# FFN-entry tensor sums moved from GpSimd to VectorE, output-projection operands split in two tiles, and mixer C's head norm moved into its attention pipeline

## The chip, the cores and the metric

The kernel runs on one core of one Trainium2 chip. A core has five engines, each with its own in-order queue of instructions: TensorE (PE in the profile; its weight loads are PEld), VectorE (DVE), ScalarE (ACT), GpSimd (POOL) and SyncE (SP), which here issues the DMAs. Engines wait for each other by semaphores. The metric is the device time of one execution in microseconds; lower is better.

## The reference

A trunk of two post-norm layers on 1024 tokens of width 1024, in float32. Layer 0 mixes with mixer AB (dilated-window attention beside latent attention), layer 1 with mixer C (differential attention, 8 heads of width 128, each normed on its own). What matters here:

```python
o = diff_attention(q, k, v, lam)                       # mixer C
o = rms_norm(o, subln, LN_EPS) * (1.0 - lambda_init)   # per head, over its 128 values
y = o.reshape(B, S, C_MIX) @ w_out
x = layer_norm(ALPHA * x + y, ln_mix_g[i], ln_mix_b[i])
a = x @ w_gate; u = x @ w_up                           # then conv over tokens, gelu, product, w_down
```

The output is the residual stream after both layers.

## The kernel before

Every float32 product is made of three matmuls in a faster float32 format: each operand is split into a high part (a cast, on ACT or POOL) and a low part (value minus high part, on DVE), and `mm3` (L157 to L160) adds high x high, high x low and low x high in PSUM. Tokens stand in 8 tiles of 128. The stages follow one another: projections and heads of mixer AB, `out_proj(0)`, `ffn(0)`, an embedding gate, then the same for layer 1 with mixer C. The code gives an order, and a scheduler reorders instructions within it before they are put in the engines' queues; from then on each engine is in order.

*Mixer C.* `pipeline` runs 8 heads of 8 items (128 queries each). In one slot it starts an item's scores and softmax (`a`: scores s on PE, maximum on DVE, exponential on ACT at L439, combination on POOL and DVE), transposes a finished one (`b`: tiles xt, copied as pth by ACT and ptl by DVE), and after every second item multiplies a pair with the values (`c`: PSUM tile av, copied by ACT into oT, the head's transposed output of 1024 columns). Beside that, projections of the next head run (pp, then nat, ks, kt and v). PE's PSUM tiles of one bank (`bank`, tag b) rotate over four banks; scores and the pair tiles of the FFN use two tiles of two banks (`banks2`). Seven heads' oT go to DRAM (mix), the last stays in SBUF.

*Output projection.* `out_proj` goes over the token tiles. For a tile it loads seven heads (`MixTiles.seven`, tile mr), copies the last head in (`last`), and splits into mh and ml. For layer 1 it first norms: `norm` squares on ACT (sq, L893), sums over the head's 128 partitions with a matmul by ones (ss, L895), takes Ln and Exp on ACT (L896, L897) and scales on DVE (L898), in pieces of 512, 384 and 128 columns. `linear` runs 2 halves n of 8 k, 48 matmuls into two one-bank tiles po, and adds each half to the residual xn on DVE (L1069). `ln` is the layer norm (statistics and two passes on DVE, L870 to L881; two tiny steps rs and mostly the last pass, L882, on POOL). `xt.put` of the tile before transposes its normed rows on PE (xt). In the last tile `linear` calls put of tile 6 and the first weight splits amid its second half; put of tile 7 follows in `ffn`.

*FFN entry.* The two FFN products are block products of 2 x 2 blocks with seven multiplications in place of eight. They need sums of the weight blocks (s1 to s4, tile ws) and of the token blocks (t1 to t4): `Weights.sums` makes s1 and s3 on POOL always, and s2 and s4 on POOL too for the first two weights; `XSeven.put` makes t1 and the raw t2 tile by tile, and `finish` makes t3 and t4 after the last tile, with the first of two sums each on DVE and the second on POOL (128x1024). All are split again. `ffn` runs the products of the first two weights interleaved (`order`), reads the results with sums on DVE (L1158: u, c), and starts the third weight when PSUM frees. Weights come by two DMAs of 512 KB each (`load`, tiles wf).

```python
order = [(0, "a00"), (0, "a01"), (1, "a00"), (1, "a01")]
order += [(m, name) for name in ("s1", "s4", "s2", "s3", "a11") for m in range(2)]
```

Of the kernel before, what the change touches and what calls it, by code (L numbers as in the profile page):

```python
# [15 lines left out]
P = 128  # L16
NT = 8
# [14 lines left out]
def tile_hybrid_encoder(  # L32
# [294 lines left out]
    class XSeven:  # L327
# [10 lines left out]
        def put(self, t, xn):  # L338
# [3 lines left out]
            if t == 4:  # L342
                self.make("t1")
                self.make("b11")
                self.t2 = [unit("t2", [P, 2, 512]) for _ in range(2)]
            if t >= 4:
                t1 = mid2("t1", [P, 4, P])

            def put(b, pt):
                for j in range(2):  # L350
# [11 lines left out]
                    if t >= 4 and b == 1:  # L362
                        add(self.t2[j][at], src, v, ALU.subtract)
            transposed(xn, put)

        def finish(self, j, temps):

            for n in ("t2", "t3", "t4"):
                self.make(n, 1)
            h, l = ({n: x[j] for n, x in d.items() if len(x) > j} for d in (self.h, self.l))  # L370
            t2, (t3, t4) = self.t2[j], temps
# [5 lines left out]
            self.t2[j] = None  # L377

            def step():
                split_value(t3, h["t3"], l["t3"])  # L380
                split_value(t4, h["t4"], l["t4"])
            return step
# [87 lines left out]
    def pipeline(items, plan):  # L470
# [9 lines left out]
        pending = None  # L480
        for i in range(n):
# [5 lines left out]
            plan.run(i, "mid")  # L487
            if pending is not None:
                pending.c()
                pending = None  # L490
# [4 lines left out]
        pending.c()  # L495

# [90 lines left out]
    class ItemA:  # L587
# [37 lines left out]

        def c(self):
# [81 lines left out]
    class ItemB:  # L708
# [30 lines left out]
        c = ItemA.c  # L739

# [75 lines left out]
    class ItemC:  # L816
# [26 lines left out]
        def c(self):  # L843
# [6 lines left out]
            nc.scalar.copy(oT[:, q4 * 256:q4 * 256 + 256], po)  # L850
# [34 lines left out]
    class MixTiles:  # L885
# [4 lines left out]
        def norm(self, x, n):  # L890

            sq = mid2("sq", [P, n, P])
            nc.scalar.activation(sq, x, AF.Square)  # L893
            pss = blocks(bank("ss"))[:, 0:n, :]
            nc.tensor.matmul(pss, lhsT=ones, rhs=sq, start=True, stop=True)  # L895
            nc.scalar.activation(sq, pss, AF.Ln, bias=eps_ln, scale=1.0 / 128)  # L896
            nc.scalar.activation(sq, sq, AF.Exp, scale=-0.5)  # L897
            nc.vector.scalar_tensor_tensor(x, x, sub, sq, op0=ALU.mult, op1=ALU.mult)  # L898
# [12 lines left out]
        def last(self, t, oT):  # L911
            mr, mh, ml = self.m[t]
            nc.scalar.copy(mr[:, 7, :], oT[:, t * P:(t + 1) * P])
            if self.i == 1:
                self.norm(mr[:, 7:8], 1)
            split(mr[:, 7:8], mh[:, 7:8], ml[:, 7:8])
            self.m[t] = mh, ml
# [126 lines left out]
    def out_proj(i, w, mt, oT, xsrc, xt, early):  # L1044
# [14 lines left out]
        def linear(t, beside):  # L1059
            mh, ml = m.pop(t)  # L1060
            xr = xns[t]
            for n in range(2):
                sl = slice(512 * n, 512 * n + 512)
                po = bank("po")
                for k in range(NK):
                    if n == 1 and k == NK // 2:
                        beside()
                    mm3(po, mh[:, k, :], ml[:, k, :], w[k][0][:, sl], w[k][1][:, sl], k == 0, k == NK - 1)
                nc.vector.scalar_tensor_tensor(xr[:, sl], xr[:, sl], ALPHA, po, op0=ALU.mult, op1=ALU.add)  # L1069

        load(0)
        for t in range(NT):
            residual(t)
            load(t + 1)
            if t == NT - 1:
                early(0)

                def beside():
                    xt.put(t - 1, xns[t - 1])
                    early(1)  # L1080
                linear(t, beside)
            else:
                linear(t, lambda: None)
                if t:
                    xt.put(t - 1, xns[t - 1])
            ln(xns[t], t >= NT - 2)
            nc.sync.dma_start(out=xmid[i][t], in_=xns[t])
# [3 lines left out]
    class Weights:  # L1091
# [13 lines left out]
        def sums(self, eng=None):  # L1105
# [7 lines left out]
            self.v.update({"a11": a11, "s1": s1, "s2": s2, "s3": s3, "s4": s4})  # L1113

# [8 lines left out]
        def steps(self):  # L1123

            return [self.sums] + [lambda n=n: self.split(n) for n in Products.ORDER]
# [435 lines left out]
```

## Time and profile before

| | |
|---|---|
| median of 3 runs | 3123.81 us (3122.83 to 3125.05) |
| profiled execution | 3123.14 us, its span 3120.8 us |
| granted TensorE clock, mean | 0.990 |
| PE, DVE, ACT, POOL busy in the span | 97%, 74%, 38%, 35% |
| mixer C, one head | 71.0 us |
| projection 1, its first matmul to its 46th of the last tile | 2209.91 to 2323.30 us |
| entry of ffn(1), up to the first output sum u | to 2381.59 us |

The profile is of one execution. A row of a group has line, engine, operation, output and inputs, shapes and count, then busy us and mean ns of one, then the idle time before it and what ended that. A timeline row has start and length in us; a bracket gives idle time just before it and what ended it. A row of the waits has who waited for whom, total us, times, and the longest.

### The profile page before, as it was taken

The numbers are of one execution on the slowest core, as the hardware profiler recorded it, in microseconds if no ns is written. First come the engines' busy times: TensorE is split into PE (matmuls) and PEld (weight loads), VectorE is DVE, ScalarE is ACT, GpSimd is POOL, SyncE is SP. The second block draws the span as 40 slices with busy tenths as digits, with TensorE's granted clock in tenths as the row PEclk, the third lists the DMA queues.
The fourth block names the chain that finished last, engine by engine and source line by source line (L and its number), as shares of the span: only waits on it lengthen the run. The fifth ranks groups of instructions, "written<-read, shape, count | busy, mean of one in ns | idle before, by whom it ended". The sixth has DMA issues, their size and how long they took to land.

```text
span 3120.8 us, 43023 instructions
## 1 busy us (share of the span) xinstructions
PE 3014.5 (97%) x15704; PEld 2589.3 (83%) x15704; DVE 2295.5 (74%) x3850; ACT 1184.5 (38%) x2506; POOL 1084.9 (35%) x1560
## 2 busy tenths in 40 slices
PE   8999999999799999999999999999898999999999
PEld 8888989888678888888889999998676888888887
DVE  6666487875898887867638777778679888877764
ACT  5555577761232222101225555555423222211111
POOL 4444544333532221101225555554344222211112
PEclk9999999999999999999999999999999999999999
DMA  3000100044122222623111010004322222243221
GB/s 120 28 28 25 31 28 8 28 132 131 69 81 81 81 81 93 217 95 108 59 63 32 28 35 28 28 18 134 105 93 75 81 81 81 81 176 135 102 78 64
DMA packets 89250, 237.50 MB, mean 76 GB/s; under 512 B 9040, under 2 KB 32720, under 8 KB 89040
## 3 DMA queue, kind: packets, MB, share of 16 engines
q1 hardware_dynamic: 89040, 234.76, 22.0%
q8 instruction: 124, 2.03, 0.3%
q14 instruction: 86, 0.70, 0.1%
HBM read 179.15 MB, written 55.57 MB: 75 GB/s over the span
## 4 chain that ended last, share of the span: by engine, by line
PE 60%; DVE 5%; DMA 2%; POOL 2%; issue 1%; ACT 1%; SPq 0%; DVEq 0%; ACTq 0%; POOLq 0%
PE pb L160 5%; PE pb L159 5%; PE pb L158 5%; PE pd L158 5%; PE pd L159 5%; PE pd L160 5%; PE s L583 4%; PE pp L159 3%; PE pp L160 3%; PE pp L158 3%; PE pa L158 2%; PE xt L163 2%; PE pa L160 2%; PE pa L159 2%; PE pg L158 2%; PE pg L160 2%
## 5 line engine op out<-in xcount | busy, mean ns | idle before, releaser
L1363 DVE TENSOR_TENSOR xn<-xn,pd 128x512 f32<-128x512 f32 x320 | 213.1, 683 | 91.9 <-PE pd L160 90.9
L141 DVE TENSOR_TENSOR ptl<-xt,pth 128x512 fp32r<-128x512 f32 (+2 forms) x384 | 239.9, 652 | 55.4 <-ACT pth L398 38.8
L158 PE MATMUL pd<-dh,dh 128*128 128x512 f32 x704 | 274.3, 390 | 2.2 <-DVE xn L1363 2.2
L158 PE MATMUL pp<-wh,xth 128*128 128x384 f32 x768 | 266.8, 348 | 8.7 <-ACT wh L145 6.8
L159 PE MATMUL pd<-dl,dh 128*128 128x512 f32 x704 | 274.0, 389 | 0.0
L160 PE MATMUL pd<-dh,dl 128*128 128x512 f32 x704 | 273.3, 389 | 0.0
L159 PE MATMUL pp<-wl,xth 128*128 128x384 f32 x768 | 260.3, 339 | 1.6 <-DVE wl L148 1.5
L160 PE MATMUL pp<-wh,xtl 128*128 128x384 f32 x768 | 259.2, 338 | 0.0
L439 ACT ACTIVATE e<-s,nmx 128x1024 f32<-128x1024 f32 x192 | 214.4, 1118 | 96.1 <-DVE nmx L829 73.1
L324 ACT CAST w<-ws 128x512 fp32r<-128x512 f32 x132 | 81.5, 621 | 355.7 <-PE pb L160 284.1
L159 PE MATMUL pb<-xt,w 128*128 128x512 f32 x528 | 207.2, 392 | 7.2 <-DVE xt L141 7.2
L158 PE MATMUL pb<-xt,w 128*128 128x512 f32 x528 | 206.8, 392 | 0.0
L160 PE MATMUL pb<-xt,w 128*128 128x512 f32 x528 | 206.4, 391 | 0.0
L163 PE MATMUL xt<-ident,e 128*128 128x128 f32 x1440 | 193.3, 273 | 5.7 <-POOL e L732 3.0
L138 POOL TENSOR_SCALAR w<-ws 128x512 fp32r<-128x512 f32 x44 | 34.9, 794 | 426.5 <-PE pa L160 403.2
L163 PEld LDWEIGHTS xt<-ident,e 128*128 128x128 f32 x1440 | 163.2, 141 | 18.7 <-POOL e L732 4.3
L324 ACT CAST dh<-dr 128x1024 fp32r<-128x1024 f32 x44 | 46.1, 1052 | 334.7 <-DMA dr<-gated 193.4
L138 POOL TENSOR_SCALAR dh<-dr 128x1024 fp32r<-128x1024 f32 x44 | 46.3, 1054 | 355.1 <-DMA dr<-in_w_down_dram 164.3
L141 DVE TENSOR_TENSOR w<-ws,w 128x512 fp32r<-128x512 f32 x176 | 160.5, 914 | 1.5 <-ACT w L324 0.5
L158 PEld LDWEIGHTS pd<-dh,dh 128*128 128x128 f32 x704 | 132.1, 188 | 30.5 <-DVE xn L1363 3.1
L158 PEld LDWEIGHTS pp<-wh,xth 128*128 128x128 f32 x768 | 145.4, 190 | 13.8 <-ACT wh L145 7.6
L160 PEld LDWEIGHTS pd<-dh,dl 128*128 128x128 f32 x704 | 132.1, 188 | 27.6
(281 smaller groups left out, 8798.7 us busy)
## 6 DMA issues: line engine op xcount, KB each, us to landing
wf<-in_w_gate_dram SPq DMA_DIRECT2D x44, 512.0 KB, 3.9
wf<-in_w_up_dram SPq DMA_DIRECT2D x44, 512.0 KB, 4.1
gated<-c SPq DMA_DIRECT2D x44, 512.0 KB, 2.9
dr<-in_w_down_dram SPq DMA_DIRECT2D x44, 512.0 KB, 3.2
dr<-gated SPq DMA_DIRECT2D x44, 512.0 KB, 3.7
wr<-in_w_c_dram SPq DMA_DIRECT2D x32, 384.0 KB, 3.2
pes<-peo SPq DMA_DIRECT2D x64, 128.0 KB, 2.1
xmid<-xn SPq DMA_DIRECT2D x16, 512.0 KB, 2.9
```

Of the source, the lines that this page charges most:

```text
L138: nc.gpsimd.tensor_scalar(o, i, 1.0, 1.0, op0=ALU.mult, op1=ALU.mult)
L141: nc.vector.tensor_tensor(lo, src, f32(hi), op=ALU.subtract)
L158: nc.tensor.matmul(o, lhsT=lh, rhs=rh, start=start, stop=False)
L159: nc.tensor.matmul(o, lhsT=lh, rhs=rl, start=False, stop=False)
L160: nc.tensor.matmul(o, lhsT=ll, rhs=rh, start=False, stop=stop)
L163: nc.tensor.transpose(o, in_=i, identity=ident)
L324: nc.scalar.copy(h, v)
L439: nc.scalar.activation(dst, s, AF.Exp, bias=negmax, scale=1.0, accum_out=l)
L583: nc.tensor.matmul(s[:, kh * 512:kh * 512 + 512], lhsT=qt[:, hl, i, :], rhs=self.ks[kh][:, j, :], start=hl == 0, stop=hl == 1)
L1363: nc.vector.tensor_tensor(xns[t][:, sl], xns[t][:, sl], po, op=ALU.add)
```

## The change

Three parts. (1) The head norm of mixer C leaves the output projection: `ItemC.c` squares the pair's result, and a new step `d`, one slot later, sums, takes Ln and Exp and scales, 256 columns at a time, 32 times. For the other mixers' items `d` does nothing. (2) In `out_proj` the split goes into two tiles of four k (high and low side by side), the last head is split straight from oT, k is the outer loop with both halves n in one two-bank tile, one DVE addition of 1024 columns takes the place of two, and every put follows the next tile's `linear`. (3) At the FFN entry all tensor sums of the first two weights and of t3 and t4 are on DVE; t3 is made tile by tile in put; the steps are spread over other places of `order`; the load of the second weight follows the split of the first. From the third weight on nothing changes.

```diff
@@ XSeven.put @@
+                self.t3 = [unit("t3", [P, 2, 512]) for _ in range(2)]
             if t >= 4:
-                t1 = mid2("t1", [P, 4, P])
+                t1, b01 = mid2("t1", [P, 4, P]), mid2("b01", [P, 4, P])
 
             def put(b, pt):
+                if t >= 4 and b == 0:
+                    nc.scalar.copy(b01, pt)
...
                     if t >= 4 and b == 1:
                         add(self.t2[j][at], src, v, ALU.subtract)
+                        add(self.t3[j][at], src, b01[:, 2 * j:2 * j + 2, :], ALU.subtract)
...
-        def finish(self, j, temps):
-
-            for n in ("t2", "t3", "t4"):
-                self.make(n, 1)
...
-            add(t3, t2, h["b00"], ALU.subtract)
-            add(t3, t3, l["b00"], ALU.subtract, nc.gpsimd)
-            add(t4, h["b10"], t2, ALU.subtract)
-            add(t4, t4, l["b10"], ALU.add, nc.gpsimd)
-            split_value(t2, h["t2"], l["t2"])
...
+        def finish(self, name, j, temp=None):
+
+            self.make(name, 1)
+            h, l = self.h[name][j], self.l[name][j]
+            if name == "t4":
+                add(temp, self.h["b10"][j], self.t2[j], ALU.subtract)
+                add(temp, temp, self.l["b10"][j])
+                v, self.t2[j] = temp, None
+            elif name == "t3":
+                v, self.t3[j] = self.t3[j], None
+            else:
+                v = self.t2[j]
+            split_value(v, h, l)
@@ pipeline @@
             plan.run(i, "mid")
+            if ended is not None:
+                ended.d()
+                ended = None
             if pending is not None:
                 pending.c()
-                pending = None
+                pending, ended = None, pending
             items[i].b()
@@ ItemC @@
-            nc.scalar.copy(oT[:, q4 * 256:q4 * 256 + 256], po)
+            o = oT[:, q4 * 256:q4 * 256 + 256]
+            nc.scalar.copy(o, po)
+            self.sq = mid2("sq", [P, 256])
+            nc.scalar.activation(self.sq, po, AF.Square)
+
+        def d(self):
+
+            oT, sq, q4 = self.st["oT"], self.sq, self.t // 2
+            o = oT[:, q4 * 256:q4 * 256 + 256]
+            pss = bank("ss")[:, 0:256]
+            nc.tensor.matmul(pss, lhsT=ones, rhs=sq, start=True, stop=True)
+            nc.scalar.activation(sq, pss, AF.Ln, bias=eps_ln, scale=1.0 / 128)
+            nc.scalar.activation(sq, sq, AF.Exp, scale=-0.5)
+            nc.vector.scalar_tensor_tensor(o, o, sub, sq, op0=ALU.mult, op1=ALU.mult)
             if self.t == NT - 1:
                 self.st["sink"](oT)
@@ MixTiles @@
-        def norm(self, x, n):
...
-            if self.i == 1:
-                self.norm(mr[:, 0:4], 4)
-                self.norm(mr[:, 4:7], 3)
-            mh, ml = runit("mh", [P, NK, P]), runit("ml", [P, NK, P])
-            split(mr[:, 0:7], mh[:, 0:7], ml[:, 0:7])
-            self.m[t] = mr, mh, ml
+            two = [runit("mhl", [P, 2, 4, P]) for _ in range(2)]
+            for j, m in enumerate(two):
+                n = 4 - j
+                split(mr[:, 4 * j:4 * j + n], m[:, 0, 0:n], m[:, 1, 0:n])
+            self.m[t] = mr, two
 
         def last(self, t, oT):
...
+            mr, two = self.m[t]
+            x = oT[:, t * P:(t + 1) * P]
+            split(x, two[1][:, 0, 3], two[1][:, 1, 3], nc.scalar)
+            self.m[t] = [(two[k // 4][:, 0, k % 4], two[k // 4][:, 1, k % 4]) for k in range(NK)]
@@ out_proj @@
+        def linear(t, beside=None):
+
+            xr, mt_ = xns[t], m.pop(t)
+            po = banks2("po")
+            for k in range(NK):
+                if k == NK // 2 and beside:
+                    beside()
+                for n in range(2):
+                    sl = slice(512 * n, 512 * n + 512)
+                    mm3(po[:, sl], *mt_[k], w[k][0][:, sl], w[k][1][:, sl], k == 0, k == NK - 1)
+            nc.vector.scalar_tensor_tensor(xr, xr, ALPHA, po, op0=ALU.mult, op1=ALU.add)
...
+            if t < NT - 1:
+                linear(t)
+            else:
                 early(0)
...
+                linear(t, lambda: early(1))
+                ln(xns[t], True)
+                nc.sync.dma_start(out=xmid[i][t], in_=xns[t])
+            if t:
+                xt.put(t - 1, xns[t - 1])
+            if t < NT - 1:
+                ln(xns[t], t == NT - 2)
+                nc.sync.dma_start(out=xmid[i][t], in_=xns[t])
@@ Weights.sums, ffn_early @@
-            add(s1, a10, a11, ALU.add, nc.gpsimd)
-            add(s2, s1, a00, ALU.subtract, eng)
-            add(s4, a01, s2, ALU.subtract, eng)
-            add(s3, a00, a10, ALU.subtract, nc.gpsimd)
             self.v.update({"a11": a11, "s1": s1, "s2": s2, "s3": s3, "s4": s4})
+            steps = [lambda: add(s1, a10, a11, ALU.add, eng), lambda: add(s2, s1, a00, ALU.subtract),
+                     lambda: add(s4, a01, s2, ALU.subtract), lambda: add(s3, a00, a10, ALU.subtract, eng)]
+            if eng is None:
+                return steps
...
                 w[0].load()
-                w[1].load()
             else:
                 w[0].split("a00")
                 w[0].split("a01")
+                w[1].load()
@@ ffn @@
-        w[0].sums(nc.gpsimd)
...
-        w[1].sums(nc.gpsimd)
...
+                for a in range(2):
+                    sums[a] = w[a].sums()
+                    sums[a][0]()
+                    w[a].split("s1")
...
+            if n == 2:
+                for a in range(2):
+                    sums[a][1]()
+                    sums[a][2]()
+                    w[a].split("s4")
             if n == 3:
...
+                for a in range(2):
+                    xt.finish("t2", a)
+                for a in range(2):
+                    w[a].split("s2", True)
             if n == 4:
...
+                for a in range(2):
+                    xt.finish("t3", a)
+                for a in range(2):
+                    sums[a][3]()
+                    w[a].split("s3")
             if n == 5:
...
+                for a in range(2):
+                    xt.finish("t4", a, temps[a])
```

How the instructions stand: PE in mixer C, in the slot after the one that finished a pair, before (xt are transposes of attention weights, s scores, kt keys):

```order
L163 MATMUL kt_18427<-ident,nat_18314 128x128
L163 MATMUL xt_18444<-ident,e_18259 128x128 x4
L163 MATMUL xt_18451<-ident,e_18259 128x128 x4
L583 MATMUL s_18459<-ks_17358,qt_18280 128x512 x2
L583 MATMUL s_18459<-ks_17754,qt_18280 128x512 x2
L583 MATMUL s_18468<-ks_17358,qt_18280 128x512 x2
```

and now:

```order
L163 MATMUL kt_18481<-ident,nat_18367 128x128
L868 MATMUL ss_18498<-sq_18404,ones 128x256
L163 MATMUL xt_18504<-ident,e_18312 128x128 x4
L587 MATMUL s_18519<-ks_17383,qt_18333 128x512
L163 MATMUL xt_18511<-ident,e_18312 128x128 x4
L587 MATMUL s_18519<-ks_17383,qt_18333 128x512
L587 MATMUL s_18519<-ks_17788,qt_18333 128x512 x2
L587 MATMUL s_18528<-ks_17383,qt_18333 128x512 x2
```

ss, the matmul by ones, stands between kt and the transposes, and one score matmul has moved between the two transposed groups. ACT in the same slot now (nat, ks and v are copies of the projection):

```order
L546 COPY nat_18487<-pp_18456 128x256
L567 CAST ks_18265<-kt_18481 64x128
L554 CAST v_18266<-pp_18456 128x128
L869 ACTIVATE sq_18404<-ss_18498,eps_ln 128x256
L398 CAST pth_18406<-xt_18504 128x4x128
L870 ACTIVATE sq_18404<-sq_18404 128x256
L567 CAST ks_18265<-kt_18481 64x128
L398 CAST pth_18407<-xt_18511 128x4x128
```

Ln (L869) and Exp (L870) stand behind the copies of the projection and around the first copy pth. POOL at the entry of ffn(1), before (ws are weight sums, wf raw weights, w the split, rs the layer norm's two steps):

```order
L318 TENSOR_TENSOR ws_24159<-wf_24057 128x512
L874 TENSOR_SCALAR rs_24044<-mv_24043 128x1
L318 TENSOR_TENSOR ws_24160<-wf_24056,wf_24057 128x512
L875 TENSOR_TENSOR rs_24044<-rs_24044,mhalf 128x1
L318 TENSOR_TENSOR ws_24159<-ws_24159,wf_24056 128x512
L318 TENSOR_TENSOR ws_24160<-wf_24056,ws_24159 128x512
L318 TENSOR_TENSOR ws_24171<-wf_24061 128x512
L318 TENSOR_TENSOR ws_24172<-wf_24060,wf_24061 128x512
L318 TENSOR_TENSOR ws_24171<-ws_24171,wf_24060 128x512
L318 TENSOR_TENSOR ws_24172<-wf_24060,ws_24171 128x512
L138 TENSOR_SCALAR w_24168<-wf_24060 128x512
L874 TENSOR_SCALAR rs_24149<-mv_24148 128x1
```

and now, from the same place:

```order
L138 TENSOR_SCALAR w_24152<-wf_24120 128x512
L895 TENSOR_SCALAR rs_24108<-mv_24107 128x1
L896 TENSOR_TENSOR rs_24108<-rs_24108,mhalf 128x1
L138 TENSOR_SCALAR w_24228<-wf_24155 128x512
L895 TENSOR_SCALAR rs_24186<-mv_24185 128x1
L896 TENSOR_TENSOR rs_24186<-rs_24186,mhalf 128x1
L138 TENSOR_SCALAR w_24378<-ws_24246 128x512
L138 TENSOR_SCALAR w_24382<-ws_24252 128x512
```

The ws rows are gone from POOL; the norm's steps follow each other. DVE shortly ahead of the first u, now (c holds t4 for a while, xb and t token blocks and their sums):

```order
L318 TENSOR_TENSOR ws_24246<-wf_24120,wf_24121 128x512
L318 TENSOR_TENSOR ws_24252<-wf_24155,wf_24156 128x512
L318 TENSOR_TENSOR c_24301<-xb_4987_23590,t_5039_23970 128x1024
L141 TENSOR_TENSOR w_24378<-ws_24246,w_24378 128x512
L141 TENSOR_TENSOR w_24382<-ws_24252,w_24382 128x512
L318 TENSOR_TENSOR c_24301<-c_24301,xb_4989_23592 128x1024
L318 TENSOR_TENSOR c_24301<-xb_4988_23591,t_5040_23971 128x1024
L141 TENSOR_TENSOR w_24427<-wf_24121,w_24427 128x512
L141 TENSOR_TENSOR xt_5115_24401<-c_24301,xt_5114_24400 128x1024
L318 TENSOR_TENSOR c_24301<-c_24301,xb_4990_23593 128x1024
L141 TENSOR_TENSOR w_24430<-wf_24156,w_24430 128x512
L141 TENSOR_TENSOR xt_5117_24407<-c_24301,xt_5116_24406 128x1024
```

The sums s3 (first two rows) and t4 stand on DVE among the low parts (L141) of the split.

More of the change, by code (lines that the diff above doesn't have):

```diff
@@ L479, in pipeline @@
         plan.run(-1, "last")
-        pending = None
+        pending = ended = None
         for i in range(n):
@@ L487, in pipeline @@
             plan.run(i, "mid")
+            if ended is not None:
+                ended.d()
+                ended = None
             if pending is not None:
                 pending.c()
-                pending = None
+                pending, ended = None, pending
             items[i].b()
@@ L495, in pipeline @@
         pending.c()
+        pending.d()
     class Block64:
@@ L624, in make_pt @@
             return PTA(self.t)
+        def d(self):
+            pass
         def c(self):
@@ L739, in tile_hybrid_encoder @@
         c = ItemA.c
+        d = ItemA.d
     class Latent:
@@ L888, in __init__ @@
             self.i, self.m = i, {}
-        def norm(self, x, n):
[L892 to L898, printed above, removed]
         def seven(self, t):
@@ L1057, in residual @@
             nc.sync.dma_start(out=xns[t], in_=xsrc[t])
[L1059 to L1069, printed above, removed]
+        def linear(t, beside=None):
[8 more added lines that the diff above has]
+            nc.vector.scalar_tensor_tensor(xr, xr, ALPHA, po, op0=ALU.mult, op1=ALU.add)
         load(0)
@@ L1074, in out_proj @@
             load(t + 1)
-            if t == NT - 1:
+            if t < NT - 1:
+                linear(t)
+            else:
                 early(0)
[L1078 to L1087, printed above, removed]
+                linear(t, lambda: early(1))
[6 more added lines that the diff above has]
+                nc.sync.dma_start(out=xmid[i][t], in_=xns[t])
         return lambda: xt.put(NT - 1, xns[NT - 1])
@@ L1108, in sums @@
             s1, s2, s3, s4 = s12[:, 0], s12[:, 1], s34[:, 0], s34[:, 1]
-            add(s1, a10, a11, ALU.add, nc.gpsimd)
-            add(s2, s1, a00, ALU.subtract, eng)
-            add(s4, a01, s2, ALU.subtract, eng)
-            add(s3, a00, a10, ALU.subtract, nc.gpsimd)
             self.v.update({"a11": a11, "s1": s1, "s2": s2, "s3": s3, "s4": s4})
+            steps = [lambda: add(s1, a10, a11, ALU.add, eng), lambda: add(s2, s1, a00, ALU.subtract),
+                     lambda: add(s4, a01, s2, ALU.subtract), lambda: add(s3, a00, a10, ALU.subtract, eng)]
+            if eng is None:
+                return steps
+            for step in steps:
+                step()
         HI = {"s3", "a01", "a11"}
@@ L1123, in steps @@
         def steps(self):
-            return [self.sums] + [lambda n=n: self.split(n) for n in Products.ORDER]
+            return [lambda: self.sums(nc.gpsimd)] + [lambda n=n: self.split(n) for n in Products.ORDER]
     class Products:
@@ L1294, in ffn @@
         order += [(m, name) for m in range(2, NF) for name in Products.ORDER]
-        w[0].sums(nc.gpsimd)
+        sums = [None] * 2
         w[1].split("a00", False)
         w[1].split("a01", False)
-        w[1].sums(nc.gpsimd)
-        first = [None] * 2
         todo = []
@@ L1303, in ffn @@
             pr[m].product(name)
-            if n == 1:
+            if n == 0:
                 c00 = unit("c00", [P, 2, 512])
@@ L1307, in ffn @@
                     pr[a].go_ahead(c00[:, a])
-                w[0].split("s1")
-                w[1].split("s1")
-            if n == 2:
+                for a in range(2):
+                    sums[a] = w[a].sums()
+                    sums[a][0]()
+                    w[a].split("s1")
+            if n == 1:
                 late()
                 new_c()
-                c2 = late_c[0]
-                first[0] = xt.finish(0, [c2[:, a, :].rearrange("p (k q) -> p k q", k=2) for a in range(2)])
+                temps = [late_c[0][:, a, :].rearrange("p (k q) -> p k q", k=2) for a in range(2)]
+            if n == 2:
[3 more added lines that the diff above has]
+                    w[a].split("s4")
             if n == 3:
-                w[0].split("s4")
-                w[1].split("s4")
-                w[0].split("s2", True)
-                w[1].split("s2", True)
+                for a in range(2):
+                    xt.finish("t2", a)
+                for a in range(2):
+                    w[a].split("s2", True)
             if n == 4:
-                first[1] = xt.finish(1, [unit("t", [P, 2, 512]) for _ in range(2)])
+                for a in range(2):
[3 more added lines that the diff above has]
+                    w[a].split("s3")
             if n == 5:
-                w[0].split("s3")
-                first[0]()
-                w[1].split("s3")
-                first[1]()
+                for a in range(2):
+                    xt.finish("t4", a, temps[a])
             if n == 6:
```

14 lines of the change are left out of this document (1 added, 13 removed).

## The prediction

> **What bounds the kernel now.** I read the page first (busy shares, the chain that ended last), then the busy time by stretch, then the waits of TensorE (PE) around the two places that the change touches, and then single rows.
>
> ```profile
> PE 3014.5 (97%) x15704; PEld 2589.3 (83%) x15704; DVE 2295.5 (74%) x3850; ACT 1184.5 (38%) x2506; POOL 1084.9 (35%) x1560
> PE 60%; DVE 5%; DMA 2%; POOL 2%; issue 1%; ACT 1%; SPq 0%; DVEq 0%; ACTq 0%; POOLq 0%
> ```
>
> PE is busy for 97% and holds 60% of the chain; no other engine has over 5% of it. The shares are averages, so I cut the span into stretches: one head of mixer C, the output projection of layer 1, and the entry of each FFN. The columns are the stretch, its length, busy us (and instructions) of PE, PE's weight loads, DVE, ACT and POOL, the granted clock, and the DMA share and rate.
>
> ```profile
> 1786.00:1857.00 71.00, 70.00 (x444) 65.87 (x441) 53.57 (x90) 39.17 (x92) 39.21 (x64) 1.00 0.10 31
> ...
> 800.00:857.00 57.00, 41.19 (x163) 32.36 (x162) 55.48 (x59) 16.82 (x28) 38.59 (x22) 0.88 0.15 56
> ...
> 2208.00:2324.00 116.00, 109.22 (x476) 85.61 (x474) 79.69 (x124) 38.04 (x94) 41.68 (x39) 0.97 0.30 101
> 2324.00:2382.00 58.00, 39.95 (x162) 31.84 (x162) 53.70 (x59) 16.23 (x27) 34.17 (x21) 0.87 0.15 55
> ```
>
> A head of mixer C is PE and nothing else: 70.00 of 71.00 us. Whatever is added to PE there is paid. In the two FFN entries it is DVE that is full (53.70 of 58.00, 55.48 of 57.00) while PE is busy for 40 us and runs at a granted clock of 0.87 to 0.88. What PE waits for there, first in 2190 to 2420, then in 690 to 905:
>
> ```profile
> PE xt L163 <- DVE xn L882: 10.9, 2, 5.5
> PE ss L895 <- DVE xb L141: 6.0, 3, 3.4
> PE pa L158 <- DVE u L1158: 4.4, 1, 4.4
> PE pb L159 <- DVE xt L141: 3.4, 2, 1.8
> ```
> ```profile
> PE xt L163 <- DVE xn L882: 8.5, 2, 6.1
> ...
> PE pa L158 <- DVE u L1158: 3.1, 1, 3.1
> PE xt L163 <- POOL xn L882: 2.8, 3, 1.3
> ```
>
> So the last two layer norms (xn), the tensor operands (xt) and the first output sum (u) come late, all from DVE. Why DVE is late stands in its own rows:
>
> ```profile
> 2350.99 0.42 DVE L141 TENSOR_TENSOR xb<-xt,xb 128x256 fp32r<-128x256 f32 x1
> 2351.33 0.41 DVE L318 TENSOR_TENSOR t<-xt,t 128x256 f32<-128x256 f32 x1
> 2351.66 1.22 DVE L318 TENSOR_TENSOR c<-t,xb 128x1024 f32<-128x1024 f32 x1
> 2352.79 1.63 DVE L318 TENSOR_TENSOR c<-xb,t 128x1024 f32<-128x1024 f32 x1
> ...
> 2356.08 3.42 DVE L318 TENSOR_TENSOR t<-t,xb 128x1024 f32<-128x1024 f32 x1
> ...
> 2371.98 0.68 DVE L141 TENSOR_TENSOR w<-ws,w 128x512 fp32r<-128x512 f32 x1
> 2372.58 2.35 DVE L141 TENSOR_TENSOR xt<-t,xt 128x1024 fp32r<-128x1024 f32 x2
> ...
> 2379.86 1.09 DVE L318 TENSOR_TENSOR ws<-ws,wf 128x512 f32<-128x512 f32 x1
> ...
> 2381.59 1.28 DVE L1158 TENSOR_TENSOR u<-m,pa 128x512 f32<-128x512 f32 x2
> ```
> ```profile
> 2356.01 5.75 POOL L318 TENSOR_TENSOR c<-c,xb 128x1024 f32<-128x1024 f32 x2
> ...
> 2379.36 1.05 POOL L138 TENSOR_SCALAR w<-wf 128x512 fp32r<-128x512 f32 x1
> ```
>
> From start to start DVE takes 0.34 us for 256 columns, 1.13 for 1024 and 0.60 for 512. The same 1024-wide sum takes 3.42 us at 2356.08, in just the 5.75 us in which POOL runs a tensor sum. A cast on POOL does less: beside the one at 2379.36 DVE takes 1.09 for 512 columns in place of 0.68, 0.4 more. So POOL's tensor sums both feed this path and slow it.
>
> **The change, term by term** (against the profiled run's 3123.14 us, a span of 3120.8 and 2.3 around it; the median of the three runs, 3123.81, is 0.7 above).
>
> *FFN entries.* From the last matmul of the last tile of the output projection to the first output sum u. In layer 1:
>
> ```profile
> 2323.30 0.39 PE L158 MATMUL po<-woh,mh 128*128 128x512 f32 x1
> 2329.04 1.94 PE L163 MATMUL xt<-ident,xn 128*128 128x128 f32 x8 [5.35 <-DVE xn L882]
> ```
>
> At 0.23 us a matmul the tile would have ended at 2323.98 had the transposes not been put in its midst, and u starts at 2381.59: 57.6 us. In layer 0 the same two marks are 800.52 and 856.42, 55.9 us:
>
> ```profile
> 800.29 0.39 PE L160 MATMUL po<-woh,ml 128*128 128x512 f32 x1
> ```
> ```profile
> 856.42 1.28 DVE L1158 TENSOR_TENSOR u<-m,pa 128x512 f32<-128x512 f32 x2
> ```
>
> After the change DVE does POOL's sums too, at its own pitch. Between the last projection sum and u its changed order has 64 instructions: 14 of 1024 columns, 25 of 512 (23 sums, splits and output sums, two of the norm's statistics), 24 of 256 and one tiny: 14 x 1.13 + 25 x 0.60 + 24 x 0.34 + 0.2 = 39.2 us, if POOL's sums no longer stretch them. PE's own work there is 144 matmuls of 0.23 and 16 transposes (about 1.7): 34.8. So DVE still sets the end. I add 2.8 us for the seven casts that POOL keeps there, at 0.4, and 2.1 for DVE's stops (POOL's steps of the last norm, the a01 and s1 products): 44.1 us. Bounds: 39.2 (none of these) and half of the gain lost. Gains: **13.5 us off** in layer 1 (6.8 to 18.4), 11.8 in layer 0 (5.9 to 16.7). The wait for u does not go; I expect 3 to 4 us of it. The loads of w[1] move behind the split of w[0]; a load of this kind lands in 4.1 us,
>
> ```profile
> wf<-in_w_up_dram SPq DMA_DIRECT2D x44, 512.0 KB, 4.1
> ```
>
> and on SP's queue it stands behind an xmid store that waits for a norm. By the order it lands about 1 us before it is needed; that slim cover, when gone, costs 2 to 3 us per entry, inside the bounds.
>
> *Output projections.* In layer 1 eight tiles of 48 matmuls at 0.2275 us plus six sets of transposes of 0.9 are 92.8 us; they take 2209.91 to 2323.98, 114.1. The 21.3 us between are the norm (the ss rows and their waits). In layer 0, with no norm, the waits in the same place are 2.8 us (three of the kind xt <- POOL xn). I leave 1.5 us: **19.8 off** in layer 1 (17 to 21), 1.0 in layer 0 (0 to 2). Two 512-wide sums become one 1024-wide one, k outside n changes no matmul, and POOL's 16 small copies (mh) of the last head go; PE hides all three.
>
> *Mixer C.* 32 ones-matmuls of 256 columns with their Square, Ln, Exp and scaling are added. Their price on PE, from the projection's own:
>
> ```profile
> 2208.27 1.89 PE L895 MATMUL ss<-sq,ones 128*128 128x512 f32 x6
> 2209.91 0.47 PE L158 MATMUL po<-woh,mh 128*128 128x512 f32 x1
> ```
>
> 1024 columns in 1.64 us, so 0.41 for 256, 0.45 with a little for each start: 32 x 0.45 = **14.4 us added**. Then the wait that comes with it. ss takes one of four PSUM banks and frees it when ACT has read it with Ln. By the changed order PE does kt, ss, four transposes and one score matmul, and then wants that bank; ACT does nat, ks and v first. Before, the same place reads:
>
> ```profile
> 1800.39 0.27 PE L163 MATMUL kt<-ident,nat 128*128 128x128 f32 x1
> 1800.50 1.04 PE L163 MATMUL xt<-ident,e 128*128 128x128 f32 x8
> ...
> 1800.64 0.37 ACT L542 COPY nat<-pp 128x256 f32<-128x256 f32 x1 [1.36 <-PE pp L160]
> 1800.91 0.26 ACT L563 CAST ks<-kt 64x128 fp32r<-64x128 f32 x1
> 1801.07 0.26 ACT L550 CAST v<-pp 128x128 fp32r<-128x128 f32 x1
> ```
>
> ss would run 1800.50 to 1800.95 with its result some 0.2 later; Ln could start at 1801.22 and take about 0.5 (0.59 for 384 columns in the next rows); PE asks for the bank at 0.95 + 0.40 + 0.23, 1801.58, and gets it at 1801.8: 0.2 us, in 24 of the 32 places (in the others ss stands where ACT is idle). 4.8 us; bounds 0 and 0.6 us each, 0 to 14. ACT (39 of 71 us) and DVE (54) have room for the rest, some 4 and 1.4 us a head.
>
> ```profile
> L896 ACT ACTIVATE sq<-ss,eps_ln 128x384 f32<-128x384 f32 x8 | 4.7, 586 | 0.0
> ...
> L1229 ACT ACT_TABLE_LOAD x1 | 1.3, 1283 | 0.0
> ```
>
> The second row answers a doubt of its own: in the whole of 2190 to 2420, where Ln, the norm's Exp and the softmax's Exp alternate, ACT loads one table, and that for the FFN's gate. So I count no loads.
>
> *Tail of mixer C.* Two groups of norm matmuls among the last products leave, the one above and this:
>
> ```profile
> 2200.17 3.32 PE L895 MATMUL ss<-sq,ones 128*128 128x512 f32 x4 [2.73 <-ACT sq L893]
> ```
>
> 5.0 us in all. But the last items' softmax chain stays, and PE then waits longer for it than these 2.73; I take 1.7 off (0 to 3).
>
> Sum: 3123.14 - 13.5 - 11.8 - 19.8 - 1.0 - 1.7 + 14.4 + 4.8 = 3094.5.
>
> **Rivals.** (1) *DVE is the bound.* With POOL's sums DVE has 39 us of work against PE's 35, so any stretching is paid in full. If the casts and norm steps that POOL keeps stretch DVE as the sums did, half of the entry gain is lost: 6.8 + 5.9, so 3107.2. For it: DVE was at 93 to 97% busy. Against: the row of 2379.86, 0.4 us beside a cast, where the sum at 2356.08 lost 2.2 beside sums.
>
> (2) *Mixer C pays more* (the slower side). PE has one bank less in hand. The softmax's exponentials take ACT 1.12 us each:
>
> ```profile
> L439 ACT ACTIVATE e<-s,nmx 128x1024 f32<-128x1024 f32 x192 | 214.4, 1118 | 96.1 <-DVE nmx L829 73.1
> ```
>
> If Ln stands behind two of them, PE waits 2.2 us at 24 places: 53 us in place of 4.8, 3142.7. The whole turns to a loss from 1.4 us a place on (28.6 + 4.8 over 24), from 1.65 beyond what can be measured. Against: in the changed order both exponentials stand ahead of nat, ks and v, a stretch of PE products earlier.
>
> (3) *The norm's waits only change their name.* Without the norm, the projection of layer 1 may wait for its input tiles or their split on POOL as long as it did for ss; layer 0, with the same loads and 2.8 us of waits, says no. If 15 of the 19.8 us stay and rival 1 holds, 3122.2.
>
> (4) *All bounds are kind*: no wait for the bank, no stops and no casts on DVE's way: 3094.5 - 4.8 - 9.8 = 3079.9.
>
> (5) *Ln and Exp do not share a table after all.* Two loads of 1.283 us (the row above) for each of 32 norms, if PE waits for all: 82.1 us, 3176.6. Against: that there is only one load in 2190 to 2420, and the changed order has eight loads in all, as before. The Trainium skill, "ScalarE: Activation LUTs", section "What ACT_TABLE_LOAD costs", speaks against such mixing: a switch between sets costs a load of about 1283 ns and a drain of about 1380, by which the 64 switches would come to 170 us. Its section "Table sets: the hidden batching unit" puts ln and exp into one set; the trace agrees with both, by the length of its load and by there being one.
>
> **How the numbers follow.** Forecast 0.56 (3094.5, by itself 3086 to 3102), rival 1 0.20, rival 2 0.06, rival 3 0.08, rival 4 0.09, rival 5 0.01. A measurement of this kernel tells about 0.2%, 6.2 us, from no change. Faster: forecast, rivals 1 and 4, a quarter of rival 3: 0.87; within 0.2%: the rest of it, 0.06; slower: rivals 2 and 5, 0.07. The range, 3078 to 3112, holds the forecast, rivals 1 and 4 and the bounds of the wait for the bank (3089.7 to 3104.1), and leaves out rivals 2, 3 and 5.
>
> **What would show it.** Right: a head of mixer C at 73.4 us in place of 71.0 (four norms of 0.45 and three waits of 0.2) with a wait xt <- ACT sq of some 0.2 us; no ss between the projections; from the last projection matmul to u 41 to 47 us, DVE's 1024-wide sums at 1.2 us throughout; the waits for xn down from 10.9 to under 3 us. Wrong: heads of 75 us or more, or an FFN entry over 50 us with DVE rows still at 2 to 3 us.

## The result, and the profile after

| | before | after |
|---|---|---|
| median | 3123.32 us (3121.79 to 3125.05, 4 runs) | 3106.85 us (3105.07 to 3107.68, 4 runs) |
| span of the profiled execution | 3120.8 us | 3104.4 us |
| after over before | | 0.9947, 95% interval 0.9931 to 0.9963 |

16.5 us faster: inside the range of 3078 to 3112, and 12.4 above the forecast of 3094.5. It is also outside 3086 to 3102, which the prediction gave for the forecast by itself, and 0.4 from the 3107.2 of its rival 1. A second set of runs, with the last experiments, gave 3107.68 us and 0.9942 (0.993 to 0.9955).

By stretch, the changed kernel: one head of mixer C, the FFN entry of layer 0 (from the end of the last projection matmul to u), the projection of layer 1, the FFN entry of layer 1. Columns as before.

```profile
1742.15:1815.26 73.11, 72.12 (x450) 67.14 (x448) 55.90 (x93) 43.10 (x104) 39.51 (x64) 1.00 0.10 30
799.47:848.45 48.98, 37.37 (x161) 29.28 (x159) 45.80 (x67) 16.76 (x29) 13.25 (x11) 0.93 0.19 65
2214.72:2314.86 100.14, 97.68 (x461) 80.86 (x459) 62.84 (x113) 15.18 (x42) 29.08 (x34) 0.99 0.33 112
2314.86:2363.68 48.82, 37.37 (x161) 29.25 (x159) 45.67 (x67) 16.77 (x29) 13.23 (x11) 0.93 0.17 65
```

A head went from 71.0 to 73.1 us, an entry from 55.9 and 57.6 to 49.0 and 48.8, and POOL from 39 and 34 to 13 us of work in an entry. DVE is still the full engine there, 45.7 of 48.8. But with 67 instructions it is busy for 45.8 and 45.7 us, where the prediction's rows of nearly the same stretches have 59 in 55.5 and 53.7: it took over POOL's sums and still needs less time. Its 1024-wide sums, up to 3.42 us beside POOL's sums before, now take 1.2 to 2.3. The waits of PE in 2190 to 2420:

```profile
PE pa L158 <- DVE u L1167: 9.1, 1, 9.1
PE xt L163 <- ACT e L439: 2.8, 1, 2.8
PE xt L163 <- POOL xn L903: 2.5, 2, 1.8
PE pb L158 <- DVE t L318: 2.0, 1, 2.0
PE xt L163 <- DVE e L845: 1.7, 1, 1.7
PE pb L158 <- DVE u L1167: 1.4, 1, 1.4
PE xt L163 <- DVE xn L903: 1.1, 2, 0.6
```

The waits for ss are all but gone (0.3 us is left) and those for xn on DVE fell from 10.9 to 1.1, but the one for u has doubled, from 4.4 to 9.1 us. So a part of what the other waits were worth collects at the first thing that DVE delivers after all of its added work.

### The profile page after: what moved, and what is told of

Same layout as the page of the kernel before. It is cut to its first block, busy times and chain, and to the rows that moved or that the text cites. A ratio compares the mean times of both kernels' runs of the same rounds, so it can differ in the third digit from the quotient of the medians.

```text
span 3104.4 us, 43067 instructions
## 1 busy us (share of the span) xinstructions
PE 3008.3 (97%) x15720; PEld 2582.7 (83%) x15720; DVE 2280.5 (73%) x3890; ACT 1186.8 (38%) x2538; POOL 1022.9 (33%) x1536
## 4 chain that ended last, share of the span: by engine, by line
PE 79%; DVE 10%; DMA 3%; ACT 2%; issue 2%; POOL 2%; SPq 0%; DVEq 0%; ACTq 0%; POOLq 0%
PE pb L159 6%; PE pb L160 6%; PE pb L158 6%; PE xt L163 5%; PE pd L158 4%; PE pd L159 4%; PE pd L160 4%; PE pp L158 4%; PE pp L160 4%; PE pp L159 4%; PE s L587 4%; PE pa L158 2%; PE pa L160 2%; PE pa L159 2%; PE pg L158 2%
## 5 line engine op out<-in xcount | busy, mean ns | idle before, releaser
L141 DVE TENSOR_TENSOR ptl<-xt,pth 128x512 fp32r<-128x512 f32 (+2 forms) x384 | 239.6, 652 | 60.3 <-ACT pth L398 43.6
L141 DVE TENSOR_TENSOR w<-ws,w 128x512 fp32r<-128x512 f32 x176 | 161.0, 918 | 4.5 <-ACT w L324 2.2
L159 PEld LDWEIGHTS pd<-dl,dh 128*128 128x128 f32 x704 | 132.2, 188 | 27.7 <-DVE dl L141 0.7
```

Source lines behind the costliest of these rows:

```text
L141: nc.vector.tensor_tensor(lo, src, f32(hi), op=ALU.subtract)
L159: nc.tensor.matmul(o, lhsT=lh, rhs=rl, start=False, stop=False)
```

## The experiments

Two kinds of mark are used below, both read from timelines: the entry is the time from the end of the last projection matmul (its start and 0.23 us) to the start of the first u; behind it comes the time from that u to the first down projection (pd). Times of kernels are compared as ratios to the kernel before on the same chip, whose median was 3125.1 (first four), 3125.3 (next four) and 3124.9 us (last four).

**The norm's move alone** (part 1 on the kernel before).

```diff
             pending.c()
+            pending, ended = None, pending
...
+        def d(self):
...
-            if self.i == 1:
-                self.norm(mr[:, 0:4], 4)
-                self.norm(mr[:, 4:7], 3)
```

> Before with part 1 alone: the head norm of mixer C in the pipeline, the output projection without it, all else as before. If the parts add up and the prices read from the changed kernel hold (32 sums by ones at 0.43 us in mixer C, +13.7 us; its tail 2.3 shorter; the projection 14 shorter), the run is 2 to 5 us faster than before. If the projection then loses all of its 21 us, as the forecast had it (20), it is 8 to 11 us faster. Rival: without the new operand tiles the projection keeps its waits under other names, and the run is slower than before by up to 10 us.

3124.81 us, ratio 1.0002 (0.9993 to 1.0011): nothing. Mixer C pays its price (73.2 us a head), and the time from the last kt of mixer C to the end of the projection falls from 193.7 to 181.3 us; in the changed kernel it is 177.4, 3.9 less. The projection itself falls from 114.1 to 96.2 us, but the tail ahead of it grows from 79.6 to 85.1. What is missing is seen in the order of the tail, further down. The time lies between the two readings (2 to 5 us faster, up to 10 us slower) and does not decide between them; by the marks the first is nearer, as the waits of the projection did go.

**The projection's new operands and order alone** (part 2, with the norm kept in the projection).

```diff
-            for n in range(2):
-                sl = slice(512 * n, 512 * n + 512)
-                po = bank("po")
-                for k in range(NK):
...
+            po = banks2("po")
+            for k in range(NK):
...
+                for n in range(2):
```

> Before with part 2 alone: operands in two tiles, k outside n, put after each linear, one wide sum; the head norm stays in the projection of layer 1. Forecast: 1 us in layer 0 and next to nothing in layer 1, but put of tile 6 no longer stands amid the last tile, so a part of the two waits for xn (5.4 and 5.5 us before) may go: 0 to 8 us faster. Rival: the order of put and linear is what shortens the entry, not the sums; then 12 us or more faster.

3123.4 us, ratio 0.9997 (0.9988 to 1.0006): nothing. The entries are 55.1 and 55.6 us against 55.9 and 57.6. So the place of put and linear hardly shortens the entry; the rival falls.

**The FFN entry alone** (part 3).

```diff
-            add(s1, a10, a11, ALU.add, nc.gpsimd)
...
+            steps = [lambda: add(s1, a10, a11, ALU.add, eng), lambda: add(s2, s1, a00, ALU.subtract),
...
-            add(t3, t3, l["b00"], ALU.subtract, nc.gpsimd)
```

> Before with part 3 alone: all tensor sums of the first two weights and of t3 and t4 on DVE, t3 made tile by tile. If POOL's sums were what held DVE up, both entries get shorter by 7 to 9 us less some 2 us given back after the longer wait for u: 10 to 14 us faster. Rival: DVE only takes over what POOL did and part 2 gave the gain: within 4 us of before.

3112.49 us, ratio 0.9961 (0.9949 to 0.9974), 12 us faster, with entries of 46.7 and 47.6 us. These are shorter than the changed kernel's, but the projections ahead of them took 2.9 and 3.5 us more than before, so the two together gain 6.3 and 6.5 us. The moved sums are two thirds to three quarters of the gain (12 of 16.5 to 18 us), as the first reading had it.

**Each sum by ones in mixer C twice.**

```diff
-            nc.tensor.matmul(pss, lhsT=ones, rhs=sq, start=True, stop=True)
+            for _ in range(2):
+                nc.tensor.matmul(pss, lhsT=ones, rhs=sq, start=True, stop=True)
```

> The changed kernel with every sum by ones in mixer C done twice into the same bank (the second overwrites the first). If PE alone pays and the bank costs nothing, 32 more of them cost 32 x 0.43 = 13.7 us over the changed kernel. If PE then waits for the bank (Ln 0.4 us later), 24 places cost 0.2 to 0.6 us more: 18 to 28 us.

3121.81 us, ratio 0.9992 (0.9983 to 1.0001); beside the changed kernel's 0.9942 some 15 us, near the first reading. A head takes 74.4 us in place of 73.1: four times 0.43 is 1.7, and 0.4 of it hides in the wait of kt for POOL's nat, which falls from 1.0 to 0.6 us a head. That is 10 of the 15 us; most of the rest lies behind the last kt, where the tail and the projection take 185.4 us in place of 177.4, and I did not follow it. The wait for the bank is there, but does not grow with the length of ss: Ln starts as much later as PE asks later. The place in the changed kernel (rows of PE, its weight loads and ACT):

```profile
1742.15 0.27 PE L163 MATMUL kt<-ident,nat 128*128 128x128 f32 x1
1742.26 0.60 PE L868 MATMUL ss<-sq,ones 128*128 128x256 f32 x2
...
1742.69 0.60 PE L163 MATMUL xt<-ident,e 128*128 128x128 f32 x4
...
1742.95 0.47 ACT L869 ACTIVATE sq<-ss,eps_ln 128x256 f32<-128x256 f32 x1
1743.05 0.47 PE L587 MATMUL s<-ks,qt 128*128 128x512 f32 x1
...
1743.48 0.42 PEld L163 LDWEIGHTS xt<-ident,e 128*128 128x128 f32 x4 [0.27 <-ACT sq L869]
1743.48 0.66 PE L163 MATMUL xt<-ident,e 128*128 128x128 f32 x4
```

ss takes 0.43 us from start to start. Behind the score matmul at 1743.05 the transposes wait for Ln, which ends at 1743.42: the bracket is on the weight load, and PE's own row shows no gap, since the matmul's modelled end covers it. Start to start, 0.43 us where 0.25 would do (eight such score matmuls took 1.96 us before): 0.2 us, as forecast. In the kernel with ss doubled:

```profile
1746.83 1.03 PE L869 MATMUL ss<-sq,ones 128*128 128x256 f32 x4
1747.70 0.60 PE L163 MATMUL xt<-ident,e 128*128 128x128 f32 x4
1748.05 0.48 PE L587 MATMUL s<-ks,qt 128*128 128x512 f32 x1
1748.49 0.66 PE L163 MATMUL xt<-ident,e 128*128 128x128 f32 x4
```

ss 0.87, and again 0.44 from the score matmul to the transposes.

**More work for DVE in the entry.**

```diff
-                add(temp, self.h["b10"][j], self.t2[j], ALU.subtract)
+                for _ in range(2):
+                    add(temp, self.h["b10"][j], self.t2[j], ALU.subtract)
```

> The changed kernel with the first of the two sums for t4 done twice (the same result): DVE gets two more sums of 128x1024 in each entry, 4 x 1.13 = 4.5 us in all. If DVE sets the end of the entry, the time grows by 4 to 6 us over the changed kernel. If PE or a transfer does, by under 1 us.

3113.91 us, ratio 0.9961 (0.9946 to 0.9976); the entries grew from 49.0 and 48.8 to 51.3 and 51.1, by 2.4 and 2.3 us for two sums of 1.13, and by the ratios the whole run by 4 to 6 us, the first reading. The one wait shows it to a tenth:

```profile
PE pa L158 <- DVE u L1168: 11.4, 1, 11.4
```

DVE sets the end of the entry, one for one; a transfer or PE does not.

**Casts from POOL to ACT.**

```diff
-            split_value(self.v[name], hl[:, 0], hl[:, 1], nc.gpsimd if name in self.HI else None)
+            split_value(self.v[name], hl[:, 0], hl[:, 1], nc.gpsimd if name in self.HI and self.f > 0 else None)
```

> The changed kernel with the high parts of a01, s3 and a11 of the first two weights cast on ACT in place of POOL (six casts of 128x512 in each entry). If DVE is stretched by what POOL still does there (its work before u took 43.5 us for 39.2 by the free pitches, some 4.3 too long), about half of that goes, the rest being the third weight's two sums on POOL: 2 to 3 us in each entry, 4 to 6 us faster than the changed kernel. Rival: the stretch is of DVE's own making or ACT's casts come late for DVE's low parts: within 2 us of it, or slower.

3103.99 us, ratio 0.993 (0.9913 to 0.9946), by the ratios 4 to 5 us faster than the changed kernel, in intervals that overlap. The entries are 48.2 and 46.8 us, 0.8 and 2.0 less; the wait for u is 7.5. An entry with the same code can differ by as much (47.6 and 47.3 us in the kernel with ss doubled), so the surer sign is DVE's busy time in the entry: 43.8 and 43.7 us in place of 45.8 and 45.7, where the kernel with ss doubled has 45.9 and 45.6. The six casts stretch DVE by 2.0 us an entry; I had put 0.4 each, 2.4.

**t4 finished later.**

```diff
-            if n == 5:
+            if n == 10:
                 for a in range(2):
                     xt.finish("t4", a, temps[a])
```

> The changed kernel with the step that finishes t4 placed five products later in the code (n of 10 in place of 5): in DVE's order the first u then stands ahead of three of the four sums and both splits of t4. If PE stands still for u only because u is queued behind t4's work, the waits of 9.1 us fall to 3 or 4 and the half clock behind them is shorter: 5 to 14 us faster than the changed kernel. If DVE's total up to the products of t4 is the bound, PE waits for t4 instead: within 3 us of it.

3103.08 us, ratio 0.9927 (0.9912 to 0.9942). The entry falls by 6 us to 42.9, and the waits change hands:

```profile
PE pa L160 <- DVE w L141: 3.8, 1, 3.8
PE pa L158 <- DVE u L1167: 2.9, 1, 2.9
```

u comes earlier, and next in DVE's queue is the low part of the third weight, for which the same product waits a little further on. From u to pd it now takes 399.6 us in both layers in place of 396.6 and 396.4, so of twice 6 us about half comes back, and some 5 to 6 reach the end by the ratios: the low side of the first reading.

**All three**: t4 later, casts on ACT, and the third weight's sums one product later.

```diff
-            for _ in range({8: 1, 10: 2, 11: 1, 12: 1, 13: 3}.get(n, 0)):
+            for _ in range({9: 1, 10: 2, 11: 1, 12: 1, 13: 3}.get(n, 0)):
```

> The changed kernel with t4 finished later, the casts of the first two weights on ACT, and the third weight's sums one product later, so that u stands ahead of them too. If the three effects are one queue's work, they add up in part: 8 to 18 us faster than the changed kernel. If moving t4 only moves the wait, 4 to 6 us as by the casts alone.

3098.4 us, ratio 0.9912 (0.9897 to 0.9927), 9 to 11 us faster than the changed kernel, so the effects add up in part: the entries are 35.0 us, no wait for the first u is left, and the wait for the third weight's low part is 4.9. A shorter entry is not all gain: of the 14 us of each, 8.6 and 8.3 come back between u and pd (405.2 and 404.7 us).

**Then the third weight's first splits ahead of t4.**

```diff
+            for _ in range({9: 1, 10: 2, 11: 1, 12: 1, 13: 3}.get(n, 0)):
+                todo.pop(0)()
             if n == 10:
                 for a in range(2):
                     xt.finish("t4", a, temps[a])
```

> The kernel of e9 with the first splits of the third weight ahead of t4 in the code. In e9 PE waits 4.9 us for the low part of that weight (w from DVE), which stands behind three sums of t4. If that wait is only a place in DVE's queue, it falls under 2 us: 3 to 8 us faster than e9, about 15 us faster than the changed kernel. If DVE's total is the bound, PE waits for t4 or the next sums instead: within 2 us of e9.

3093.93 us, ratio 0.9903 (0.9889 to 0.9917): the fastest, 13.7 us below the changed kernel on the same chip (3107.68), and about 3 us below the one before by the ratios, in intervals that overlap. The wait for the third weight's low part is down to 0.2 us, so it was a place in DVE's queue. DVE around the first u there, and the entry by stretch:

```profile
2340.19 1.22 DVE L318 TENSOR_TENSOR c<-xb,t 128x1024 f32<-128x1024 f32 x1
2341.33 1.28 DVE L141 TENSOR_TENSOR w<-ws,w 128x512 fp32r<-128x512 f32 x2
2342.53 1.28 DVE L141 TENSOR_TENSOR w<-wf,w 128x512 fp32r<-128x512 f32 x2
2343.74 0.68 DVE L1167 TENSOR_TENSOR u<-m,pa 128x512 f32<-128x512 f32 x1
```
```profile
2308.69:2343.74 35.05, 32.27 (x140) 25.38 (x139) 32.51 (x59) 15.52 (x28) 0.96 (x3) 0.95 0.24 85
```

POOL works for 1 us in the entry and these rows of DVE are at their free lengths. The largest single wait for u that PE keeps is 2.1 us.

**t4 later still.**

```diff
-            if n == 10:
+            if n == 11:
                 for a in range(2):
                     xt.finish("t4", a, temps[a])
```

> As the one before, with t4 finished one product later still. If work of DVE can go on being moved behind what PE waits for, a little faster than that one, 0 to 3 us; if the products that need t4 are late by then and the gate behind them, slower than it by 2 us or more.

3106.2 us, ratio 0.9937 (0.9924 to 0.9951), 12 us slower than the one before. In this kernel the sums of t4 are written into a buffer that the gate of the first channels has begun to fill, so a part of these gate values is lost; the instructions on every engine are the same in number. PE now waits 3.6 us for ACT's copy m, 2.2 for w and 3.3 for xt: the work moved back is late itself, the second reading.

**The change without the norm's move** (parts 2 and 3), beside the changed kernel itself. Against the changed kernel:

```diff
-            self.sq = mid2("sq", [P, 256])
-            nc.scalar.activation(self.sq, po, AF.Square)
...
+            if self.i == 1:
+                self.norm(mr[:, 0:4], 4)
+                self.norm(mr[:, 4:7], 3)
```

> The changed kernel itself, on the chip and beside the runs of the next three, as their yardstick: 0.993 to 0.996 of before.

> Parts 2 and 3 without part 1: the head norm stays in the output projection. Part 1 alone gave nothing, parts 2 and 3 alone 0 and some 12 us. If the parts add up, this one is 0.4% faster than before and 3 to 4 us slower than the changed kernel. If part 1 only pays beside the new projection (its waits gone, the tail filled), it is 5 us or more slower than the changed kernel; if the norm's move is worth nothing there either, within 2 us of it.

3113.64 us, ratio 0.996 (0.9946 to 0.9973), against 0.9942 (0.993 to 0.9955) of the changed kernel beside it: 6.0 us slower on the medians, in intervals that overlap, so on the medians the second reading. The marks say the same: from the first kt of mixer C to the end of the projection it takes 713.4 us, and 707.9 with part 1; in the kernel with part 1 alone 712.4, where the one before took 710.3. So part 1 is worth nothing alone and some 6 us beside parts 2 and 3. One share of this: with the norm left in the projection, the time from the last kt to the projection's end is 196.6 us there (195.5 with part 2 alone), where the kernel before took 193.7. The rest is seen in the order. The tail of mixer C in the kernel with part 1 alone, and in the changed one (PE):

```profile
2222.68 1.97 PE L163 MATMUL xt<-ident,e 128*128 128x128 f32 x8 [1.70 <-DVE e L845]
2224.47 0.58 PE L158 MATMUL av<-pth,v 128*128 128x256 f32 x1
2225.44 0.58 PE L159 MATMUL av<-ptl,v 128*128 128x256 f32 x1 [0.39 <-DVE ptl L141]
```
```profile
2213.25 1.82 PE L163 MATMUL xt<-ident,e 128*128 128x128 f32 x8 [1.70 <-DVE e L845]
2214.72 0.78 PE L158 MATMUL po<-woh,mhl 128*128 128x512 f32 x1
2215.30 0.41 PE L158 MATMUL av<-pth,v 128*128 128x256 f32 x1
2215.51 0.63 PE L159 MATMUL po<-wol,mhl 128*128 128x512 f32 x1
```

With a tile of its own for the first four heads and k outside n, the projection's first tile starts among the last products (av): the wait of 0.39 us for ptl goes, and the other av run behind it at the full clock, 0.12 us from start to start at a granted clock of 1.00, in place of 0.21 at 0.50. The wait of 1.70 us for e stays. The tile's other half waits for the last head. By the code that needs both: operands that are ready before the last head is (part 2), and heads normed before that (part 1). I read this from the order and the marks (177.4 against 181.3 us up to the projection's end); I ran neither the split of operands alone beside part 1 nor part 1 with part 3 and without part 2, so that part 2 is what makes part 1 pay is not shown by a run.

## Why the prediction was right, and where its sum was off

*Mixer C: right.* Forecast 73.4 us a head with a wait for Ln of 0.2; measured 73.1, with 0.43 us for ss in place of 0.45 and the wait of 0.2. Rivals 2 and 5 did not come: Ln stands behind the copies of the projection and not behind the exponentials, as the order said, and the changed kernel loads a table eight times, as before.

*Mixer C, its tail and the projection of layer 1 together: right in sum, and in part by luck.* From the first kt of mixer C to the end of the projection it was 1613.64 to 2323.98, 710.3 us, and is 1607.00 to 2314.86, 707.9: 2.5 off, where the four terms gave 2.3 (19.8 + 1.7 - 14.4 - 4.8). That it agrees to 0.2 us is luck: up to the last kt, 13.7 us were added where the two prices of mixer C give 15.6 for the 26 of 32 norms that stand there, and behind it 16.2 came off where 17.9 should have, so that two misses of about 2 us cancel. The tail's and the projection's terms cannot be told apart as I had them, because tail and projection now overlap: the 100.1 us of the projection's stretch hold the last av and ss, so its own 19.8 was not seen as such. Rival 3 falls by the list of waits: in place of ss only the 2.5 us for POOL's last norm pass is left, and I had 1.5. In layer 0 the 1.0 us that I took off the projection did not come: it took 96.3 us before and after.

*The FFN entries: right in kind, too small in price.* I gave DVE 39.2 us of work and 4.9 for casts and stops, 44.1; it took 48.8 and 49.0, which is outside my 41 to 47, and its 1024-wide rows were not at 1.2 us throughout. The gains were 8.8 and 6.9 in place of 13.5 and 11.8: 9.6 of the missing 12.4 us. The rows of layer 1, DVE and then POOL:

```profile
2315.87 1.21 DVE L903 TENSOR_TENSOR xn<-xn,lngb 128x1024 f32<-128x1024 f32 x1
2317.00 1.21 DVE L1077 SCALAR_TENSOR_TENSOR xn<-xn,po 128x1024 f32<-128x1024 f32 x1
...
2321.39 0.81 DVE L901 TENSOR_SCALAR xn<-xn,mv,rs 128x1024 f32<-128x1024 f32 x1 [0.65 <-POOL rs L896]
...
2337.08 0.69 DVE L141 TENSOR_TENSOR w<-ws,w 128x512 fp32r<-128x512 f32 x1 [1.08 <-ACT w L324]
2338.55 1.23 DVE L141 TENSOR_TENSOR xt<-t,xt 128x1024 fp32r<-128x1024 f32 x1 [0.77 <-ACT xt L324]
...
2350.46 1.63 DVE L318 TENSOR_TENSOR c<-c,xb 128x1024 f32<-128x1024 f32 x1
...
2354.16 2.30 DVE L141 TENSOR_TENSOR xt<-c,xt 128x1024 fp32r<-128x1024 f32 x1
2356.39 2.28 DVE L318 TENSOR_TENSOR c<-c,xb 128x1024 f32<-128x1024 f32 x1
...
2363.68 1.28 DVE L1167 TENSOR_TENSOR u<-m,pa 128x512 f32<-128x512 f32 x2
```
```profile
2348.95 3.61 POOL L138 TENSOR_SCALAR w<-wf 128x512 fp32r<-128x512 f32 x3
2353.78 1.61 POOL L318 TENSOR_TENSOR ws<-wf 128x512 f32<-128x512 f32 x1 [1.21 <-DVE c L318]
2355.34 2.25 POOL L318 TENSOR_TENSOR ws<-wf,wf 128x512 f32<-128x512 f32 x1
```

Three sizes are off. First, I let DVE's 39.2 us begin at the last matmul: the projection's sum starts at 2317.00, 2.1 us after the last matmul's end, because DVE is still in the norm of tile 6; I had not counted that. Second, the stops: 46.68 us from there to u with 43.53 busy is 3.15 idle, against 2.1, most of it waiting for ACT's casts (1.08 and 0.77), which I had not named. Third, the stretch: 43.5 busy for 39.2 of free work is 4.3, against 2.8. I had counted POOL's seven casts and overlooked the two sums for the third weight, which stand ahead of u (2353.78 and 2355.34 above) and which stretch 1024 columns of DVE to 2.3 us. The list of POOL's instructions ahead of the prediction ends before them: what left POOL there are the sums of the first two weights. 2.1 + 1.05 + 1.5 is 4.7, the miss in one entry. This is rival 1's mechanism (DVE is the bound, and POOL still stretches it) at three quarters of rival 1's price (9.6 of 12.7 us); the run with two more sums shows the bound one for one. No engine waits for a load in either entry, so the slim cover of the second weight's load held.

*The wait for u: wrong.* I expected 3 to 4 us of it to stay; it is 9.1. The total hides this, as most of it is the same 4.7 us by which u came late, seen from PE. Around the end of the gap the granted clock is at half for a while:

```profile
2360.22:2370.46 10.24, 5.95 (x14) 4.48 (x15) 9.61 (x14) 1.84 (x4) 2.92 (x2) 0.50 0.01 2
```

From u to pd it was 394.8 and 395.6 us and is 396.6 and 396.4: 1.8 and 0.9 given back, 2.7 in all, which the sum lacked. The length of the gap and the half clock behind it do not settle this. Here 6.0 us of PE's work ran at half clock, in the profile of the run beside the last experiments 3.0 (its clock was 0.50 from 2355.28 to 2365.52, the gap ended at 2362.50), and the times are 396.4 and 396.5 us, the same; with the wait for u at 11.4 us it is 396.7 and 396.6; and the kernel with part 1 alone, whose wait is 2.8, takes 396.2 and 397.1. The lists of waits show 0.5 us more in each layer for the next u and for ACT's copy m behind it; where the rest of the 2.7 comes from stays open.

4.9 + 4.7 from the entries, 2.7 behind them and 1.0 from the projection of layer 0 are 13.3 us, against a miss of 12.4 on the medians and 11.7 between the profiled executions (3106.23 and 3094.5). Stretches that the change left alone differ by 1 to 2 us between the two profiles (from the last pd of layer 0 to the first kt of mixer C, 120.7 and 119.2), so the account is no closer than that.

## What to carry to other kernels

When work is moved from one engine to another that is already full in a stage, price the stage by the receiving engine's queue: everything that stands ahead of the first result that the bound engine waits for, the receiver's backlog at the stage's start included. Order is then worth a look: here t4 alone, moved behind that result, gave some 5 to 6 us, and t4 and the third weight's steps reordered, with six casts moved to ACT, gave 13.7 us, beside 16.5 for the whole change. Judge such a move by the total and not by the first result, since half or more of what the entries lost came back behind it. And parts that are worth nothing alone may be worth something together, as part 1 was beside parts 2 and 3.

## What the runs showed of the hardware

A wait that the profile shows only on the weight load (0.27 us at 1743.48, with no gap on PE's own row) is real: matmul rows carry a modelled end that covers it, and starts must be subtracted to see it. A row of 1024 columns on DVE took 1.21 us alone, 1.63 beside POOL's casts (2350.46) and 2.28 to 2.30 beside POOL's sums (2354.16, 2356.39). Around the end of the 9.1 us gap the granted clock was 0.50 for 10.24 us in two profiles of the same kernel, and 6.0 us of it in one and 3.0 in the other fell after PE had work again.
